# A decoder trunk on one core: sum steps tied to the eighth last low part, attention outputs stored from SyncE's queue, later stick-breaking heads ahead in the order, sums of x two items sooner

## The chip, the cores and the metric

The kernel runs on one core of one Trainium2 chip. The metric is device time in microseconds (us); several executions are timed and the median is taken. One more execution is recorded by the hardware profiler. The core has a matmul engine (PE, its weight loads listed as PEld), a vector engine (DVE), an activation engine (ACT), GpSimd (POOL) and SyncE (SP). SP and POOL issue nearly all DMA transfers, each on a queue of its own (q1 and q0 in the profile), and all transfers run on the same 16 DMA engines.

## The reference, cut to what matters

One layer over 512 tokens of width 1024: three causal attentions side by side, gated, merged and projected, then a squared-ReLU MLP of width 4096 with a gated input embedding; both halves end in a LayerNorm over `alpha * x + ...`. All in 32-bit floats.

```python
def mixer(x, w_in, ...):
    proj = x @ w_in
    (da_q, da_k, da_v, sb_q, sb_k, sb_v, dl_q, dl_k, dl_v, gates) = jnp.split(proj, _split_points(), axis=-1)
    ...
    merged = (g[:, :, 0] * (o_da @ w_branch_da) + g[:, :, 1] * (o_sb @ w_branch_sb)
              + g[:, :, 2] * (o_dl @ w_branch_dil))
    return merged @ w_out

def stick_breaking_attention(q, k, v):
    ...
        z = jnp.einsum('bhqd,bhkd->bhqk', qi, kt).astype(jnp.float32) * scale
        log_keep = jnp.where(before, jax.nn.log_sigmoid(-z), 0.0)
        later = lax.cumsum(log_keep, axis=3, reverse=True) - log_keep
        a = jnp.where(before, jnp.exp(jax.nn.log_sigmoid(z) + later), 0.0)
        return jnp.einsum('bhqk,bhkd->bhqd', a.astype(vt.dtype), vt)

x = LayerNorm(alpha * x + mixer(x))
x = LayerNorm(alpha * x + MLP(x) + sigmoid(x W_g) * (p W_p))
```

## The kernel before

**Products.** Each 32-bit operand is split into a high part, rounded to the matmul's own type, and a low part, the rest. A product is three matmuls: high by high, high by low, low by high (L87 to L89, L562 to L564). Most large products use a seven-product form in the manner of Strassen, for which sums of weight blocks and sums of x are needed.

**Weights.** SP loads raw chunks of 128x1024 (L213, function `fill`) into six `raw` buffers. `split_next` takes each chunk apart: ACT copies the high part (`wh`, L262), DVE subtracts for the low part (`wl`, L264), into rings of five buffers each. `then_add` (L176) lets POOL accumulate a second source onto a raw chunk by DMA.

**Sums of weights.** `sum_steps` forms the sums in DRAM (`vsum`, `qsum`, `msum`, `bsum`, `gsum`, `usum`, `dsum`): 208 steps, each a DMA on POOL, a plain copy (L1241) or an accumulating one (L1239); a step that reads or adds to a sum waits for the step before it on that sum. What spreads them over the run is twofold. In program order, the main loop goes over 321 items (an item is one product with its eviction) and adds to a credit the item's size times its rate; whenever the credit reaches 1, the next step is written down. And each step gets a dependency on `marks[0]`, the oldest of the last low parts noted in `split_next`: with `maxlen=4`, the fourth last.

**Order.** The program order is set by this loop, by generators that are stepped once or twice per item (`pending`, the heads), and by a scheduler that orders each engine's instructions by dependencies and priority. POOL, SP, ACT and DVE each work through their own list in order. `slot` hands out work buffers from a pool; a new tile in a buffer that a DMA store still reads waits for that store.

**The stages around the change.** The three attentions' projections come first; in the third one's value products (about 170 to 230 us) the sums of x (`mixer_forms`: `u7`, `u6`, `u4`, `u5`, casts at L291 and L292) begin at item `forms_at`, and value tiles (`values`) are stored to DRAM by POOL at L519. Eight stick-breaking heads run beside the products (`sb_head`): per key block Abs, Exp and Ln on ACT (L1812 to L1814), a combination on DVE (L1815), its high and low part `sph` (L1818, on ACT for heads 4 to 7) and `spl` (L1819), then on PE the sum over later keys by products with a triangle and with ones (L1844, L1849), and at last Exp (`a`, L1855), `ah` (L1858) and `al` (L1859). `put_away` (L664) stores each of eight attention outputs (`oT4` to `oT11`, 256 KB each) to DRAM from POOL; `bring_back` loads them on SP ahead of the branches. After the branches (about 435 to 620 us) come the output projection (`wout`, L1033 to L1035), whose eviction adds the residual `xn` (loaded by POOL, L1015, used at L1041), the first LayerNorm (its `lr` partly on POOL, L996), and the MLP.

Of the kernel before, what the change touches and what calls it, by code (L numbers as in the profile page):

```python
# [55 lines left out]
def trunk(tc, a, out):  # L56
    nc = tc.nc
    es = ExitStack()
    with es:
# [14 lines left out]
        def slot(name, dt=F32):  # L74
            return big.tile([P, 512], dt, name=nm(name), tag="s", bufs=NSLOT)
# [74 lines left out]
        RING, RAW = 5, 6  # L150
        ORDERED, AHEAD = 17, 4
        loads, chunks, placed = [], [], []
        lows = deque(maxlen=4)
        marks = deque(maxlen=4)
        st = {"dma": 0, "split": 0, "ring": 0}

        def load(src, w, own=False):
# [80 lines left out]
        def split_next():  # L238
            c = chunks[st["split"]]
            w, off = c["w"], c.get("off", 0)  # L240
            if c.get("pre"):
                c["pre"]()
            st["ring"] += not c.get("aside")
            if c.get("apart"):
                hs, ls = [[slot(n, F32R) for _ in range(2)] for n in ("wh", "wl")]
                parts = [(hs[i], ls[i], 512 * i, 512 * i + 512) for i in range(2)]
                c["h"], c["l"] = Halves(hs), Halves(ls)
            elif c.get("beside"):
                h, lo = c["beside"]["tiles"]
                parts = [(h[:, 512:512 + w], lo[:, 512:512 + w], 0, w)]  # L250
                c["h"], c["l"] = parts[0][:2]
            elif c.get("dst") is None:
                h = ring.tile([P, 1024], F32R, name=nm("wh"), tag="wh", bufs=RING)
                lo = ring.tile([P, 1024], F32R, name=nm("wl"), tag="wl", bufs=RING)
                parts = [(h[:, :w], lo[:, :w], 0, w)]
                c["h"], c["l"] = parts[0][:2]
                c["tiles"] = h, lo
            else:
                parts = c["dst"]
            for h, lo, a0, a1 in parts:  # L260
                raw = c["from"]["raw"][:, off + a0:off + a1]
                i = nc.scalar.copy(h, raw)  # L262
                st["cast"] = getattr(i, "ins", i)
                i = nc.vector.tensor_sub(lo, raw, h.bitcast(F32))  # L264
                st["low"] = getattr(i, "ins", i)
                lows.append(st["low"])
                marks.append(st["low"])
            for t in (c["from"], *c.get("also", ())):
                t["uses"] -= 1
            if c.get("then"):  # L270
                c["then"]()
            st["split"] += 1
# [388 lines left out]

        def put_away(k):
            kept_oT[k] = dram.tile([P, 512], F32, name=f"oT{k}")
            nc.gpsimd.dma_start(kept_oT[k], oT.pop(k), max_dma_last_dim=4096)  # L664

        def bring_back(i):
            for k in range(4 * i, 4 * i + 4):
# [60 lines left out]
        def seven(forms, operand, bank_of, done):  # L728

            cs = {}  # L730
            for p in (1, 2, 7, 6, 4, 5, 3):
                for r in range(2):
                    if not r:
                        cs[p] = [operand(cs, p, kp) for kp in range(2)]

                    def mm(ps, p=p, r=r):
                        q = slice(r * P, r * P + P)
                        for k in range(4):
                            c = cs[p][k // 2]
                            n = slice(k % 2 * 512, k % 2 * 512 + 512)  # L740
                            h, lo = forms[p][k]
                            go, end = k == 0 and p in bank_of["first"], k == 3 and p in bank_of["last"]
                            nc.tensor.matmul(ps, h[:, q], c["h"][:, n], start=go, stop=False, skip_group_check=True)  # L743
                            nc.tensor.matmul(ps, h[:, q], c["l"][:, n], start=False, stop=False, skip_group_check=True)  # L744
                            nc.tensor.matmul(ps, lo[:, q], c["h"][:, n], start=False, stop=end, skip_group_check=True)  # L745

                    def bank(p=p, r=r):
                        return bank_of["get"](p, r)

                    def ev(ps, p=p, r=r):  # L750
                        with tc.high_priority():
                            done(ps, p, r)
                    if p == 5:
                        bank_of.get("sums", set()).add(len(items))
                    item(cs[p] if r else [], mm, ev, need=cs[p], bank=bank, size=0.5)
                    items[-1]["rate"] = 1.0

        msum = [[[dram.tile([P, 1024], F32, name=f"msum{n}_{m}_{i}") for i in range(2)] for m in range(2)]
                for n in range(3)]
# [128 lines left out]
        def branch_seven(i, behind):  # L888

            s, b, cs = {}, {}, {}  # L890
            for p in (2, 1, 7, 6, 4, 5, 3):
                for r in range(2):
# [128 lines left out]
        def wout_items():  # L1021
            for half in range(2):
                cs = [chunk(a["wo"][half, c].rearrange("p k n -> p (k n)"), 1024) for c in range(4)]
                for tt in range(4):
# [12 lines left out]
                    def ev(ps, tt=tt, half=half):  # L1037
# [747 lines left out]

        ready = set()

        def sb_head(hd):
            pr, side = hd // 2, hd % 2
            rs = (A, B)[side]  # L1790
# [11 lines left out]
            w = [512, 384, 512]  # L1802
            sph, spl, later = {}, {}, {}
            for bi in (2, 1, 0):
                n = w[bi]
                ps = bank[bi][:, :n]
                e = slot("e")[:, :n]
                with ExitStack() as behind:
                    if hd == 0 and bi == 2:

                        behind.enter_context(tc.issue_after(st["cast"]))
                    nc.scalar.activation(e, ps, AF.Abs)  # L1812
                nc.scalar.activation(e, e, AF.Exp, scale=-1.0)
                ln = nc.scalar.activation(e, e, AF.Ln, bias=1.0)  # L1814
                nc.vector.scalar_tensor_tensor(e, ps, 0.0, e, op0=OP.max, op1=OP.add)  # L1815
                h = slot("sph", F32R)[:, :n]
                lo = slot("spl", F32R)[:, :n]
                (nc.scalar.copy if hd > 3 else nc.vector.tensor_copy)(h, e)  # L1818
                low = nc.vector.tensor_sub(lo, e, h.bitcast(F32))  # L1819
                if hd == 0:  # L1820

                    tie[:] = [getattr(i, "ins", i) for i in (ln, low)]
                sph[bi], spl[bi] = h, lo

                if bi == 2:
                    later[2] = (256, (h[:, HC], lo[:, HC]))
                    sm = slot("sm")[:, HB]
                    nc.vector.tensor_add(sm, e[:, HB], e[:, HC])
                    hl = slot("smp", F32R)
                    nc.vector.tensor_copy(hl[:, HB], sm)  # L1830
                    nc.vector.tensor_sub(hl[:, HC], sm, hl[:, HB].bitcast(F32))
                    later[1] = (256, (hl[:, HB], hl[:, HC]))
                elif bi == 1:
                    nc.vector.tensor_add(e[:, 128:384], e[:, 128:384], sm)
                    h = slot("smh", F32R)[:, :n]
                    lo = slot("sml", F32R)[:, :n]
                    nc.vector.tensor_copy(h, e)
                    nc.vector.tensor_sub(lo, e, h.bitcast(F32))
                    later[0] = (384, (h, lo))
                yield  # L1840
            ah, al = {}, {}
            for kb, bi, c0, n in reversed(blk):
                for hl in (sph, spl) if kb != 2 else ():
                    nc.tensor.matmul(bank[bi][:, :w[bi]], tri_r, hl[bi], start=False, stop=False,  # L1844
                                     skip_group_check=True)
# [12 lines left out]
                (nc.scalar.copy if hd > 3 else nc.vector.tensor_copy)(h, e)  # L1858
                nc.vector.tensor_sub(lo, e, h.bitcast(F32))  # L1859
                ah[bi], al[bi] = h, lo  # L1860
                if kb != 1:
                    yield
# [506 lines left out]
```

## Time and profile before

| | us |
|---|---|
| runs | 1039.46, 1041.79, 1690.32 |
| median | 1041.79 |
| profiled execution | 1041.55 |
| its span, first to last instruction | 1039.8 |
| PE busy | 1019.6 |
| DVE busy | 795.2 |
| ACT busy | 614.1 |
| POOL busy | 213.2 |

The mean granted clock of PE was 0.995. POOL's DMA queue took a share of 51.9% of the 16 DMA engines over the span with 137.18 MB, SP's 35.9% with 136.90 MB. A row of the timeline reads: start, busy time, engine, line, operation, output from input, shape, count, and in brackets the idle time of the engine before it with what ended it. A row of windows reads: window, length, then busy time and count of PE, PEld, DVE, ACT and POOL, the granted clock, the share of the DMA engines and GB/s.

### The profile page before, as it was taken

The numbers are of one execution on the slowest core, as the hardware profiler recorded it, in microseconds if no ns is written. First come the engines' busy times: TensorE is split into PE (matmuls) and PEld (weight loads), VectorE is DVE, ScalarE is ACT, GpSimd is POOL, SyncE is SP. The second block draws the span as 40 slices with busy tenths as digits, with TensorE's granted clock in tenths as the row PEclk, the third lists the DMA queues.
The fourth block names the chain that finished last, engine by engine and source line by source line (L and its number), as shares of the span: only waits on it lengthen the run. The fifth ranks groups of instructions, "written<-read, shape, count | busy, mean of one in ns | idle before, by whom it ended". The sixth has DMA issues, their size and how long they took to land.

```text
span 1039.8 us, 15638 instructions
## 1 busy us (share of the span) xinstructions
PE 1019.6 (98%) x5626; PEld 880.2 (85%) x5626; DVE 795.2 (76%) x1411; ACT 614.1 (59%) x1055; POOL 213.2 (21%) x319
## 2 busy tenths in 40 slices
PE   9999999899999999999999989999999999999997
PEld 7888887688999898888888778788999899899886
DVE  7888679687666876886788795798778777777975
ACT  7565566665444565656654743676666556566651
POOL 1322430112233113111212131221211112111001
PEclk9999999989999999999999999999999999999999
DMA  8999995678899989788999996579999999999722
GB/s 310 297 313 275 260 262 154 199 196 264 278 292 339 255 237 279 202 214 262 334 269 258 301 365 193 122 218 334 343 325 337 323 329 325 343 314 286 248 82 81
DMA packets 79373, 275.99 MB, mean 265 GB/s; under 512 B 9816, under 2 KB 10600, under 8 KB 79296
## 3 DMA queue, kind: packets, MB, share of 16 engines
q0 software_dynamic: 38352, 137.18, 51.9%
q1 hardware_dynamic: 40368, 136.90, 35.9%
q8 instruction: 44, 0.72, 0.3%
q10 hardware_dynamic: 576, 0.92, 0.2%
q14 instruction: 33, 0.27, 0.1%
HBM read 267.59 MB, written 116.42 MB: 369 GB/s over the span
## 4 chain that ended last, share of the span: by engine, by line
PE 77%; DVE 8%; DMA 7%; issue 4%; ACT 3%; POOL 1%; DVEq 0%; SPq 0%; POOLq 0%; ACTq 0%
PE mm L87 9%; PE mm L89 9%; PE mm L88 9%; PE at L1422 4%; PE at L1423 4%; PE at L1424 4%; DVE wl L264 2%; PE at L89 2%; PE at L88 2%; PE at L87 2%; PE mm L743 1%; PE mm L745 1%; PE mm L744 1%; DMA raw<-bsum 1%; DMA raw<-usum 1%
## 5 line engine op out<-in xcount | busy, mean ns | idle before, releaser
L264 DVE TENSOR_TENSOR wl<-raw,wh 128x1024 fp32r<-128x1024 f32 (+1 forms) x274 | 330.3, 1215 | 117.1 <-ACT wh L262 116.1
L262 ACT CAST wh<-raw 128x1024 fp32r<-128x1024 f32 (+1 forms) x274 | 283.6, 1041 | 213.4 <-PE mm L88 99.6
L87 PE MATMUL mm<-xhT,wh 128*128 128x512 f32 (+1 forms) x254 | 95.5, 376 | 0.0
L89 PE MATMUL mm<-xhT,wl 128*128 128x512 f32 (+1 forms) x254 | 94.4, 372 | 0.0
L88 PE MATMUL mm<-xlT,wh 128*128 128x512 f32 (+1 forms) x254 | 94.1, 370 | 0.0
L1422 PE MATMUL at<-wh,hh 128*128 128x512 f32 x188 | 73.7, 392 | 0.0
L1423 PE MATMUL at<-wl,hh 128*128 128x512 f32 x188 | 73.7, 392 | 0.0
L87 PE MATMUL mm<-x1hT,wh 128*128 128x256 f32 x256 | 72.8, 285 | 0.7 <-ACT up L1350 0.7
L1424 PE MATMUL at<-wh,hl 128*128 128x512 f32 x188 | 73.1, 389 | 0.0
L88 PE MATMUL mm<-x1lT,wh 128*128 128x256 f32 x256 | 72.4, 283 | 0.0
L89 PE MATMUL mm<-x1hT,wl 128*128 128x256 f32 x256 | 72.4, 283 | 0.0
L89 PEld LDWEIGHTS mm<-xhT,wl 128*128 128x128 f32 x254 | 47.9, 188 | 8.2
L87 PEld LDWEIGHTS mm<-xhT,wh 128*128 128x128 f32 x254 | 47.9, 189 | 7.8 <-PE mm L596 0.2
L88 PEld LDWEIGHTS mm<-xlT,wh 128*128 128x128 f32 x254 | 47.9, 189 | 7.5
L1239 POOL DMA_DIRECT2D usum<-in_wu_dram x32 | 27.6, 861 | 129.4 <-DVE wl L264 49.0
L87 PEld LDWEIGHTS mm<-x1hT,wh 128*128 128x128 f32 x256 | 48.9, 191 | 2.7 <-ACT up L1350 0.9
L88 PEld LDWEIGHTS mm<-x1lT,wh 128*128 128x128 f32 x256 | 48.9, 191 | 1.5
L89 PEld LDWEIGHTS mm<-x1hT,wl 128*128 128x128 f32 x256 | 48.9, 191 | 0.0
L1239 POOL DMA_DIRECT2D dsum<-in_wd_dram x28 | 23.4, 836 | 118.5 <-DVE wl L264 49.9
L1424 PEld LDWEIGHTS at<-wh,hl 128*128 128x128 f32 x188 | 35.3, 188 | 7.7
L1422 PEld LDWEIGHTS at<-wh,hh 128*128 128x128 f32 x188 | 35.5, 189 | 6.1
L1423 PEld LDWEIGHTS at<-wl,hh 128*128 128x128 f32 x188 | 35.5, 189 | 5.7
(677 smaller groups left out, 2868.8 us busy)
## 6 DMA issues: line engine op xcount, KB each, us to landing
usum<-in_wu_dram POOLq DMA_DIRECT2D x48, 512.0 KB, 9.4
dsum<-in_wd_dram POOLq DMA_DIRECT2D x42, 512.0 KB, 8.8
raw<-usum SPq DMA_DIRECT2D x32, 512.0 KB, 8.6
raw<-dsum SPq DMA_DIRECT2D x28, 512.0 KB, 7.7
raw<-in_wt_dram SPq DMA_DIRECT2D x26, 512.0 KB, 7.3
raw<-in_wd_dram SPq DMA_DIRECT2D x25, 512.0 KB, 6.9
raw<-in_wu_dram SPq DMA_DIRECT2D x24, 512.0 KB, 8.3
qsum<-in_wq_dram POOLq DMA_DIRECT2D x18, 512.0 KB, 9.0
```

The source lines that it names most:

```text
L87: nc.tensor.matmul(ps, wh, xh, start=start, stop=False, skip_group_check=True)
L88: nc.tensor.matmul(ps, wh, xl, start=False, stop=False, skip_group_check=True)
L89: nc.tensor.matmul(ps, wl, xh, start=False, stop=stop, skip_group_check=True)
L262: i = nc.scalar.copy(h, raw)
L264: i = nc.vector.tensor_sub(lo, raw, h.bitcast(F32))
L743: nc.tensor.matmul(ps, h[:, q], c["h"][:, n], start=go, stop=False, skip_group_check=True)
L744: nc.tensor.matmul(ps, h[:, q], c["l"][:, n], start=False, stop=False, skip_group_check=True)
L745: nc.tensor.matmul(ps, lo[:, q], c["h"][:, n], start=False, stop=end, skip_group_check=True)
L1239: i = nc.gpsimd.dma_start(o, i, accum_op=OP.add, max_dma_last_dim=4096)
L1422: nc.tensor.matmul(ps, h[:, q], c["h"][:, s], start=go, stop=False, skip_group_check=True)
L1423: nc.tensor.matmul(ps, h[:, q], c["l"][:, s], start=False, stop=False, skip_group_check=True)
L1424: nc.tensor.matmul(ps, lo[:, q], c["h"][:, s], start=False, stop=end, skip_group_check=True)
```

## The change

Five edits, with no arithmetic added or removed. A sum step depends on the eighth last low part in place of the fourth last. `put_away` no longer issues its store from POOL at once: a generator waits two steps and issues it from SP. The rates change: the items of the seven-product projections from 1.0 to 0.9, those of the branches from 1.0 to 0.7, the output projection's from 1.0 to 2.4. The ACT and DVE work of heads 4 to 7 is written under a raised priority. The sums of x begin at six items ahead of the value stage in place of four.

```diff
-        lows = deque(maxlen=4)
-        marks = deque(maxlen=4)
+        marks = deque(maxlen=8)
...
-                lows.append(st["low"])
                 marks.append(st["low"])
...
         def put_away(k):
             kept_oT[k] = dram.tile([P, 512], F32, name=f"oT{k}")
-            nc.gpsimd.dma_start(kept_oT[k], oT.pop(k), max_dma_last_dim=4096)
+
+            def later():
+                t = oT.pop(k)
+                for _ in range(2):
+                    yield
+                nc.sync.dma_start(kept_oT[k], t)
+            pending.append(later())
...
                     item(cs[p] if r else [], mm, ev, need=cs[p], bank=bank, size=0.5)
-                    items[-1]["rate"] = 1.0
+                    items[-1]["rate"] = 0.9
...
                     item([cs[p]] if r else [], mm, ev, need=[cs[p]], bank=bank, size=0.25)
-                    items[-1]["rate"] = 1.0
+                    items[-1]["rate"] = 0.7
...
                     item(cs if tt == 3 else [], mm, ev, need=cs, bank=at_bank)
+                    items[-1]["rate"] = 2.4
...
+        def ahead(hd):
+            return tc.high_priority() if hd > 3 else ExitStack()
+
         def sb_head(hd):
...
             for bi in (2, 1, 0):
-                n = w[bi]
...
+                with ahead(hd):
+                    n = w[bi]
...
-                nc.scalar.activation(e, bank[bi][:, :n], AF.Exp)
                 h = slot("ah", F32R)[:, :n]
                 lo = slot("al", F32R)[:, :n]
-                (nc.scalar.copy if hd > 3 else nc.vector.tensor_copy)(h, e)
-                nc.vector.tensor_sub(lo, e, h.bitcast(F32))
+                with ahead(hd):
+                    nc.scalar.activation(e, bank[bi][:, :n], AF.Exp)
+                    (nc.scalar.copy if hd > 3 else nc.vector.tensor_copy)(h, e)
+                    nc.vector.tensor_sub(lo, e, h.bitcast(F32))
...
-        forms_at = pair_at[0] - 4
+        forms_at = pair_at[0] - 6
```

In the diff's first loop the whole body of the head's block (Abs, Exp, Ln, the combination, `sph`, `spl` and the sums over keys) moves under `with ahead(hd)`, unchanged.

The lists of the engines show what moves. ACT at the start of the third attention's value products, before: `e_376` and `sph_377` belong to one block of a later head, `wh_394` and `wh_399` are high parts of the weights, `u4h` and `u5h` sums of x.

```order
L291 CAST u4h_365_1837<-xr_359_1808 128x512
L291 CAST u4h_367_1841<-xr_360_1810 128x512
L262 CAST wh_394_1951<-raw_236_1251 128x1024
L1812 ACTIVATE e_376_1880<-at_375_1867 128x512
L262 CAST wh_399_1961<-raw_280_1457 128x1024
L1813 ACTIVATE e_376_1880<-e_376_1880 128x512
L1814 ACTIVATE e_376_1880<-e_376_1880 128x512
L1818 CAST sph_377_1885<-e_376_1880 128x512
L291 CAST u5h_381_1894<-xr_304_1580 128x512
L291 CAST u5h_383_1898<-xr_305_1582 128x512
L569 COPY dl_v_386_1915<-mm_385_1902 128x512
```

The same place on ACT in the changed kernel, where the block's names are `e_380` and `sph_381`:

```order
L1867 ACTIVATE a_370_1847<-at_317_1621 128x512
L1868 CAST ah_371_1848<-a_370_1847 128x512
L1821 ACTIVATE e_380_1888<-at_379_1875 128x512
L1822 ACTIVATE e_380_1888<-e_380_1888 128x512
L1823 ACTIVATE e_380_1888<-e_380_1888 128x512
L1827 CAST sph_381_1893<-e_380_1888 128x512
L261 CAST wh_394_1951<-raw_236_1251 128x1024
L261 CAST wh_399_1961<-raw_280_1457 128x1024
L567 COPY dl_v_386_1915<-mm_385_1902 128x512
```

The block's four instructions stand ahead of both weight casts, and the sums of x have moved to earlier in the list.

POOL at the value stores of the same stage, before (`msum` steps are sums of gate weights, `oT6` is an attention output):

```order
L176 DMA raw_280_1457<-in_wv_dram 128x1024
L176 DMA raw_292_1520<-in_wv_dram 128x1024
L1239 DMA msum0_1_1_98<-in_wgm_dram 128x1024
L519 DMA values0_92<-dl_v_408_1995 128x512
L664 DMA oT6_2011<-oT_342_1741 128x512
L519 DMA values0_92<-dl_v_416_2035 128x512
L1241 DMA msum1_0_0_99<-in_wgm_dram 128x1024
```

And POOL there in the changed kernel:

```order
L1244 DMA msum0_1_1_98<-in_wgm_dram 128x1024
L1246 DMA msum1_0_0_99<-in_wgm_dram 128x1024
L175 DMA raw_280_1457<-in_wv_dram 128x1024
L1246 DMA msum1_1_0_101<-in_wgm_dram 128x1024
L175 DMA raw_296_1527<-in_wv_dram 128x1024
L1246 DMA bsum2_0_111<-in_wbq_dram 128x1024
L517 DMA values0_92<-dl_v_408_1995 128x512
L517 DMA values0_92<-dl_v_416_2034 128x512
```

The accumulating step of `msum0_1_1` now precedes both chunk additions, three plain copies precede the value stores, and the `oT6` store is gone from POOL; on SP it stands between two loads of raw chunks (`raw_445` and `raw_462`).

POOL at the first LayerNorm, before (`lr` is a LayerNorm's factor for one block of tokens, `dsum` sums of the MLP's second weights):

```order
L996 TENSOR_TENSOR lr_1396_6591<-lr_1396_6591,mhalf_272 128x1
L996 TENSOR_TENSOR lr_1401_6631<-lr_1401_6631,mhalf_272 128x1
L176 DMA raw_1353_6371<-in_wg_dram 128x1024
L996 TENSOR_TENSOR lr_1412_6695<-lr_1412_6695,mhalf_272 128x1
L1241 DMA dsum1_3_158<-dsum1_1_156 128x1024
L176 DMA raw_1377_6529<-in_wg_dram 128x1024
L1239 DMA dsum1_3_158<-in_wd_dram 128x1024
L996 TENSOR_TENSOR lr_1420_6741<-lr_1420_6741,mhalf_272 128x1
```

And there in the changed kernel:

```order
L1246 DMA dsum2_0_159<-in_wd_dram 128x1024
L1246 DMA dsum2_2_161<-in_wd_dram 128x1024
L1000 TENSOR_TENSOR lr_1396_6593<-lr_1396_6593,mhalf_272 128x1
L1000 TENSOR_TENSOR lr_1401_6633<-lr_1401_6633,mhalf_272 128x1
L1246 DMA usum4_0_135<-in_wu_dram 128x1024
L175 DMA raw_1353_6367<-in_wg_dram 128x1024
L1000 TENSOR_TENSOR lr_1412_6697<-lr_1412_6697,mhalf_272 128x1
L175 DMA raw_1377_6531<-in_wg_dram 128x1024
L1244 DMA dsum2_0_159<-in_wd_dram 128x1024
L1000 TENSOR_TENSOR lr_1420_6743<-lr_1420_6743,mhalf_272 128x1
```

The copy and the add of `dsum1_3` stand earlier, ahead of the LayerNorm; the add ahead of the last `lr` now belongs to a sum whose copy precedes the first `lr`. Ahead of the eight `xn` loads, earlier in POOL's list, the steps from `dsum1_0`'s add to `usum3_3`'s copy all depend on one low part, where before each had one of its own.

More of the change, by code (lines that the diff above doesn't have):

```diff
@@ L1804, in sb_head @@
             for bi in (2, 1, 0):
-                n = w[bi]
[L1806 to L1837, printed above, removed]
-                    nc.vector.tensor_sub(lo, e, h.bitcast(F32))
-                    later[0] = (384, (h, lo))
+                with ahead(hd):
+                    n = w[bi]
+                    ps = bank[bi][:, :n]
+                    e = slot("e")[:, :n]
+                    with ExitStack() as behind:
+                        if hd == 0 and bi == 2:
+                            behind.enter_context(tc.issue_after(st["cast"]))
+                        nc.scalar.activation(e, ps, AF.Abs)
+                    nc.scalar.activation(e, e, AF.Exp, scale=-1.0)
+                    ln = nc.scalar.activation(e, e, AF.Ln, bias=1.0)
+                    nc.vector.scalar_tensor_tensor(e, ps, 0.0, e, op0=OP.max, op1=OP.add)
+                    h = slot("sph", F32R)[:, :n]
+                    lo = slot("spl", F32R)[:, :n]
+                    (nc.scalar.copy if hd > 3 else nc.vector.tensor_copy)(h, e)
+                    low = nc.vector.tensor_sub(lo, e, h.bitcast(F32))
+                    if hd == 0:
+                        tie[:] = [getattr(i, "ins", i) for i in (ln, low)]
+                    sph[bi], spl[bi] = h, lo
+                    if bi == 2:
+                        later[2] = (256, (h[:, HC], lo[:, HC]))
+                        sm = slot("sm")[:, HB]
+                        nc.vector.tensor_add(sm, e[:, HB], e[:, HC])
+                        hl = slot("smp", F32R)
+                        nc.vector.tensor_copy(hl[:, HB], sm)
+                        nc.vector.tensor_sub(hl[:, HC], sm, hl[:, HB].bitcast(F32))
+                        later[1] = (256, (hl[:, HB], hl[:, HC]))
+                    elif bi == 1:
+                        nc.vector.tensor_add(e[:, 128:384], e[:, 128:384], sm)
+                        h = slot("smh", F32R)[:, :n]
+                        lo = slot("sml", F32R)[:, :n]
+                        nc.vector.tensor_copy(h, e)
+                        nc.vector.tensor_sub(lo, e, h.bitcast(F32))
+                        later[0] = (384, (h, lo))
@@ L1854, in sb_head @@
                 e = slot("a")[:, :n]
-                nc.scalar.activation(e, bank[bi][:, :n], AF.Exp)
                 h = slot("ah", F32R)[:, :n]
                 lo = slot("al", F32R)[:, :n]
-                (nc.scalar.copy if hd > 3 else nc.vector.tensor_copy)(h, e)
-                nc.vector.tensor_sub(lo, e, h.bitcast(F32))
+                with ahead(hd):
+                    nc.scalar.activation(e, bank[bi][:, :n], AF.Exp)
+                    (nc.scalar.copy if hd > 3 else nc.vector.tensor_copy)(h, e)
+                    nc.vector.tensor_sub(lo, e, h.bitcast(F32))
                 ah[bi], al[bi] = h, lo
```

## The prediction

> **What bounds the kernel now.** I read the head of the page and the chain of waits first, then a table of windows over the span, then the timeline of PE wherever a window shows it short of work, and last the timelines of ACT, DVE and POOL just ahead of those places.
>
> ```profile
> span 1039.8 us, 15638 instructions
> PE 1019.6 (98%) x5626; PEld 880.2 (85%) x5626; DVE 795.2 (76%) x1411; ACT 614.1 (59%) x1055; POOL 213.2 (21%) x319
> PE 77%; DVE 8%; DMA 7%; issue 4%; ACT 3%; POOL 1%; DVEq 0%; SPq 0%; POOLq 0%; ACTq 0%
> ...
> 170.00:180.00 10.00, 8.67 (x39) 6.56 (x38) 8.52 (x13) 6.91 (x12) 1.42 (x2) 1.00 0.60 184
> 583.00:606.00 23.00, 19.98 (x88) 15.23 (x87) 16.77 (x21) 16.36 (x25) 3.37 (x5) 1.00 1.04 338
> 1014.00:1039.80 25.80, 18.96 (x96) 16.02 (x95) 15.13 (x35) 4.99 (x12) 4.48 (x6) 0.92 0.22 82
> ```
>
> The matmul engine is busy for 1019.6 of 1039.8 us. The change removes no matmul (the instruction counts of PE are equal in both kernels), so all that it can win is PE's idle time, 20.2 us, and matmuls that ran at a lowered clock. In a windows row the figures are the window, its length, then busy time of PE, PE loads, DVE, ACT and POOL with counts, the granted clock, the DMA share and GB/s. The last row holds 25.80 - 18.96 = 6.8 us of that idle time, in the final LayerNorm, which nothing in the change touches. Some 13 us are left, and they lie in few places: the third attention's value stage around 170 to 209 us, the branches (23.00 - 19.98 = 3.0 us) and one wait behind the first LayerNorm, shown below. The rows of PE in the value stage name the waits:
>
> ```profile
> 177.83 0.50 PE L1844 MATMUL at<-sph,tri_r 128*128 128x512 f32 x1 [1.05 <-ACT sph L1818]
> 178.56 0.50 PE L1844 MATMUL at<-spl,tri_r 128*128 128x512 f32 x1 [0.23 <-DVE spl L1819]
> 194.48 0.50 PE L1844 MATMUL at<-sph,tri_r 128*128 128x512 f32 x1 [0.88 <-ACT sph L1818]
> 203.55 0.50 PE L562 MATMUL mm<-wh,u5h 128*128 128x512 f32 x1 [0.49 <-ACT wh L262]
> 204.81 0.50 PE L563 MATMUL mm<-wl,u5h 128*128 128x512 f32 x1 [0.76 <-DVE wl L264]
> 208.07 0.79 PE L562 MATMUL at<-wh,u4h 128*128 128x512 f32 x1 [2.31 <-DVE dl_v L575]
> ```
>
> The bracket is idle time and what ended it: 5.72 us in all. The lowered clock comes with the last three:
>
> ```profile
> 188.00:192.00 4.00, 4.00 (x20) 3.36 (x20) 3.85 (x7) 3.88 (x6) 2.61 (x5) 1.00 0.84 153
> 204.00:208.00 4.00, 1.01 (x4) 0.48 (x3) 4.00 (x7) 2.98 (x6) 0.52 (x1) 0.79 0.52 171
> 208.00:212.00 4.00, 3.92 (x9) 3.14 (x10) 1.63 (x5) 0.96 (x2) 0.00 (x0) 0.50 0.55 222
> ```
>
> After a window in which PE worked 1.01 us of 4, the granted clock is 0.50 and 9 matmuls fit where 20 did before. Those 9 need 9 x 4.00 / 20 = 1.8 us at the full clock, so the dip costs about 3.92 - 1.8 = 2.1 us beyond the idle time.
>
> **The change part by part.** *Head order and earlier sums of x, first wait.* The head's chain on ACT is Abs, Exp, Ln and the cast to sph, each 0.6 us.
>
> ```profile
> 172.73 1.05 ACT L262 CAST wh<-raw 128x1024 fp32r<-128x1024 f32 x1 [2.27 <-PE at L564]
> 173.68 0.59 ACT L1812 ACTIVATE e<-at 128x512 f32<-128x512 f32 x1
> 174.17 1.04 ACT L262 CAST wh<-raw 128x1024 fp32r<-128x1024 f32 x1
> 177.16 0.62 ACT L1818 CAST sph<-e 128x512 fp32r<-128x512 f32 x1 [0.76 <-DVE e L1815]
> ```
>
> Before, ACT sits 2.27 us behind a weight cast that waits for a ring buffer, and Abs stands behind it. After, the four stand ahead of both casts, and PE's two triangle products stand some 10 us later. Both wh casts now start at most four activations (2.4 us) later; the ring of five covers that if they are ready when the buffer comes free, which the 2.27 us of waiting allows. I take the whole 1.28 us (1.05 + 0.23) as won; bounds 0 and 1.28. At 194.48 three more products, 3 x 0.23 = 0.7 us by the spacing of 20 in 4.00 us, stand ahead of the waiting one: -0.7, bounds 0 and -0.88.
>
> *Stores of attention outputs and value stores.* What makes 203 to 208 late is seen on ACT, DVE and POOL:
>
> ```profile
> 187.76 1.17 POOL L1239 DMA_DIRECT2D msum<-in_wgm_dram  x1
> 189.69 0.58 POOL L519 DMA_DIRECT2D values<-dl_v  x1 [0.77 <-DVE dl_v L572]
> 190.49 0.57 POOL L664 DMA_DIRECT2D oT<-oT  x1 [0.22 <-issue]
> 191.20 0.54 POOL L519 DMA_DIRECT2D values<-dl_v  x1
> ...
> 198.61 0.62 ACT L1858 CAST ah<-a 128x512 fp32r<-128x512 f32 x1 [2.71 <-DMA values<-dl_v]
> 199.93 0.69 DVE L1859 TENSOR_TENSOR al<-a,ah 128x512 fp32r<-128x512 f32 x1 [4.17 <-DMA oT<-oT]
> 201.30 0.60 ACT L1812 ACTIVATE e<-at 128x512 f32<-128x512 f32 x1 [2.06 <-DMA values<-dl_v]
> ```
>
> ACT and DVE want buffers from the slot pool that stores still read: 2.71 + 2.06 us of ACT and 4.17 us of DVE. Everything queued behind them, the casts and low parts of the next chunks among them, comes late, and PE with them. How long transfers took in this stretch (queue, count, size, us to landing):
>
> ```profile
> raw<-in_wv_dram SPq DMA_DIRECT2D x4, 512.0 KB, 6.5
> msum<-in_wgm_dram POOLq DMA_DIRECT2D x4, 512.0 KB, 10.0
> values<-dl_v POOLq DMA_DIRECT2D x2, 256.0 KB, 9.4
> oT<-oT POOLq DMA_DIRECT2D x1, 256.0 KB, 9.3
> ```
>
> Stores of 256 KB on POOL's queue took 9.3 us, loads of twice the size on SP's 6.5. After, the accumulating msum step stands ahead of this place, where the DMA share was 0.60, and only a plain copy and the chunk's own add are still issued just ahead of the value stores; the oT store leaves POOL. I estimate that it lands 9.3 - 6.5 = 2.8 us sooner and the value stores about 2 us sooner (a copy in place of an add ahead of them, taken as a fifth of msum's 10.0 us). That takes 2.0 of the 3.56 us (0.49 + 0.76 + 2.31) from PE: -2.0, bounds 0 and -3.56. For the clock dip I take half, -1.1, bounds 0 and -2.1.
>
> The Trainium skill, "TensorE: Matmul & The Clock Gate", section Part 1 on the HAM clock gate, says that the gate knows half and full alone and falls after a whole window of about 3.4 us without enough work. By that rule the term is all or nothing: the sum would be 1.1 us higher with the dip kept, 1.0 us lower with it gone. The 0.50 above agrees with its half; no row shows the threshold.
>
> *What SP's queue pays.* Eight issues move to SP: it issues the oT store between two weight loads, and is itself in order, so a store that waits for its oT would hold the loads. By the two-step delay the outputs are written before SP comes there; SP's issue takes 0.33 us as its loads' do, and 256 KB at 6.5 / 2 is about 3.3 us of its queue, once per store. Loads run up to six raw buffers ahead, which covers it: 0, bounds 0 and +2 (one of them uncovered by 2 us). POOL's 0.57 us per store goes, off any path.
>
> *Marks and rates.* A sum step waits for the eighth last low part in place of the fourth, so it may start about four chunks earlier; the rates give the branches fewer steps and the output projection more. Where DMA is full and PE busy this moves nothing: 0, bounds -1 and +3 (a chunk's 1.05 us cast late three times). In the branches, loads of summed weights took longest:
>
> ```profile
> raw<-bsum SPq DMA_DIRECT2D x2, 512.0 KB, 14.7
> usum<-in_wu_dram POOLq DMA_DIRECT2D x2, 512.0 KB, 9.6
> ```
>
> By the marks counted in the code, one step fewer runs ahead of the branches' last loads, but four then come together. I take -0.5 of the 3.0 us, bounds +2 and -3.0.
>
> *First LayerNorm.* POOL computes the last lr behind an accumulating step that waits for its copy:
>
> ```profile
> 669.76 0.15 DVE L995 TENSOR_SCALAR lr<-lr 128x1 f32<-128x1 f32 x1
> 670.22 0.85 POOL L1239 DMA_DIRECT2D dsum<-in_wd_dram  x1 [4.42 <-DMA dsum<-dsum]
> 670.80 0.86 POOL L996 TENSOR_TENSOR lr<-lr,mhalf 128x1 f32<-128x1 f32 x1
> 675.58 0.50 PE L1161 MATMUL at<-wh,x1hT 128*128 128x512 f32 x1 [1.09 <-ACT x1r L1083]
> ```
>
> After, the add there belongs to a copy that POOL issues ahead of the first lr, so lr starts at 669.91, 0.9 us sooner: -0.9, bounds 0 and -1.09. Behind it the weight casts are next in line.
>
> Sum: -1.3 - 0.7 - 2.0 - 1.1 + 0 + 0 - 0.5 - 0.9 = -6.5 us. The profiled execution took 1041.55 us (1039.8 span and 1.75 around it), which is 0.24 us under the median of 1041.79; so 1041.55 - 6.5 = 1035.05, said as 1035.
>
> **The rivals.** *The stores land no sooner.* All 16 DMA engines stood at a share of 0.84 at 188 to 192 and more after it; if the share and not the queue sets the landing, 199.93 and 201.30 stay, and with them the terms of 2.0 and 1.1: 1035 + 3.1 = 1038. Against it speaks that 512 KB on SP's queue were faster beside them. The Trainium skill, "DMA: Bandwidth & Descriptors", section "Issuing engines are not separate DMA queues", speaks for it: starting transfers from several engines saves only the time to start them.
>
> *Slower: POOL's burst ahead of the projection's inputs.* POOL works in order, and the steps around the output projection now hang on one low part, the one of 593.57, and come in a row ahead of the xn loads.
>
> ```profile
> 590.17 1.23 DVE L264 TENSOR_TENSOR wl<-raw,wh 128x1024 fp32r<-128x1024 f32 x1 [0.78 <-ACT wh L262]
> 593.57 1.23 DVE L264 TENSOR_TENSOR wl<-raw,wh 128x1024 fp32r<-128x1024 f32 x1 [2.17 <-ACT wh L262]
> 607.22 3.26 POOL L1015 DMA_DIRECT2D xn<-in_xn_dram  x6
> 621.72 0.69 DVE L1041 SCALAR_TENSOR_TENSOR xn<-xn,at 128x512 f32<-128x512 f32 x1
> ```
>
> Two chained waits stand there: an add for its copy, a copy for its add. At 9.6 us each the first xn is issued at 594.8 + 19.2 = 614.0, against 607.22, and with the 9.6 lands at 623.6, 1.9 us after 621.72; one product of the projection (about 6 us, the distance of two such evictions) covers that. At 14.7 us each it is issued at 624.2 and lands at 638.9, 17.2 late, and 17.2 - 6 = 11 us reach PE: 1035 + 11 = 1046. It decides once xn lands after 628. For it: the DMA share of 1.04 there. Against it: loads of 14.7 us were two, and sums in the same stretch took 9.6.
>
> *Nothing moves in sum*: the heads wait for something else by the same amount, each term above at its zero end: 1041.5.
>
> **How the numbers follow.** The forecast has a chance of 0.58, stores no sooner 0.20, the burst 0.15, nothing in sum 0.07. The likeliest gives 1035. Every gain at its end would be 1.28 + 0.88 + 3.56 + 2.1 + 1.0 + 3.0 + 1.09 = 12.9, or 1028.6, which needs all at once, so the range begins at 1030; it ends at 1044, where the zero ends and half of the +2 and +3 lie, and leaves out the burst and some 0.03 below. A change within 2% is about what a measurement of this kernel can't tell from none. A gain of over 2% (21 us) is more than all the idle time that is open: 0.01. Within 2%: 0.96; slower by over 2%: 0.03, a part of the burst.
>
> **What would show it.** Right: no wait for sph or spl near 178; no wait of ACT or DVE for a store of oT near 200; PE's 208 wait under 1.5 us and no 4 us window at clock 0.50; the last lr starting right behind DVE. Wrong: the same buffer waits at the same length; a wait of DVE for xn and PE idle between 610 and 650; ACT waiting for raw where it did not, after a store on SP's queue.

## The result: slower by 1.1%, and the profile after

| | before | changed |
|---|---|---|
| median, us | 1040.55 | 1053.16 |
| lowest, us | 1039.39 | 1047.85 |
| span of the profiled execution, us | 1039.8 | 1052.9 |
| its PE busy time, us | 1019.6 | 1022.7 |

The ratio is 1.0112, with a 95% interval of 1.0075 to 1.0148: slower, by about 12 us. The forecast was 1035 us with a range of 1030 to 1044. Both medians are of five executions, the three listed above among those of the kernel before; the one of 1690.32 us is left out of the ratio, which compares undisturbed executions.

The head of the changed kernel's page:

```profile
span 1052.9 us, 15652 instructions
PE 1022.7 (97%) x5626; PEld 883.4 (84%) x5626; DVE 795.1 (76%) x1411; ACT 615.1 (58%) x1055; POOL 207.7 (20%) x311
PE 75%; DMA 12%; issue 5%; DVE 4%; ACT 2%; POOL 1%; DVEq 0%; POOLq 0%; ACTq 0%
```

The work is the same, but transfers (DMA) have grown from 7% to 12% of the chain that ended last. The span is 13.1 us longer; PE is busy for 3.1 us more with the same number of matmuls, so these ran slower, and idle for 10.0 us more. The main rows of PE's timeline with idle time ahead of them, in the changed kernel:

```profile
133.77 0.80 PE L1878 MATMUL at<-ah,sb_v 128*128 128x512 f32 x1 [5.33 <-DVE ah L1868]
171.92 0.47 PE L87 MATMUL mm<-xhT,wh 128*128 128x512 f32 x1 [2.13 <-DVE dl_k L343]
206.38 0.22 PE L1805 MATMUL at<-mask_b,identb 128*128 128x128 bf16 x1 [0.98 <-ACT dl_v L567]
355.65 0.77 PE L2108 MATMUL at<-pt,dl_vh 128*128 128x256 f32 x1 [7.62 <-DMA dl_vh<-values]
637.49 0.63 PE L947 MATMUL mm<-ident,graw 128*128 128x128 f32 x4 [0.62 <-DVE ml L952]
682.36 0.66 PE L1075 MATMUL at<-ident,xn 128*128 128x128 f32 x4 [1.45 <-ACT ple L1112]
```

The waits for `sph` near 178 and for the weights near 204 are gone, and so are the waits of 3.0 us in the branches (the 0.62 us at 637 is another one, as the experiments show). But two waits stand at places where PE did not wait before: 5.33 us for `ah` and 7.62 us for `dl_vh`, 13 us together. Each is followed by a stretch of lowered clock, as the windows show (the third figure from the end is the granted clock):

```profile
128.00:132.00 4.00, 0.44 (x2) 0.02 (x1) 0.00 (x0) 0.08 (x1) 1.87 (x4) 0.98 0.75 255
132.00:136.00 4.00, 2.23 (x6) 1.61 (x7) 2.68 (x4) 0.00 (x0) 2.62 (x5) 0.50 0.84 186
136.00:140.00 4.00, 4.00 (x15) 3.27 (x14) 3.32 (x8) 0.51 (x1) 2.29 (x3) 0.67 0.92 198
...
352.00:356.00 4.00, 0.34 (x1) 0.38 (x2) 0.00 (x0) 0.00 (x0) 0.85 (x2) 0.50 1.05 314
356.00:360.00 4.00, 4.00 (x14) 3.47 (x14) 0.00 (x0) 0.00 (x0) 0.00 (x0) 0.50 0.90 301
```

**What PE waited for.** Both waits lead to POOL. `rv` is a small bias table that ACT leaves in the work buffer `rvs` and POOL stores to DRAM in five pieces; DVE needs that buffer for `ah` and waits until the stores have read it. In the changed kernel's timeline, DVE first and then POOL:

```profile
133.29 0.43 DVE L1868 CAST ah<-a 128x512 fp32r<-128x512 f32 x1 [8.87 <-DMA rv<-rvs]
...
114.01 0.83 POOL L1244 DMA_DIRECT2D qsum<-in_wq_dram  x1 [11.05 <-DMA qsum<-qsum]
122.37 0.54 POOL L1246 DMA_DIRECT2D qsum<-qsum  x1 [4.28 <-DMA qsum<-in_wq_dram]
125.52 0.52 POOL L1246 DMA_DIRECT2D qsum<-qsum  x1 [2.62 <-DMA qsum<-in_wq_dram]
126.03 2.04 POOL L1673 DMA_DIRECT2D rv<-rvs  x4
```

The brackets of POOL are the point. It waits 11.05 us for a copy of `qsum` to land before it may issue an add to it, then 4.28 and 2.62 us more for such chains, and only then comes to `rv`. Before, the five stores stood ahead of those sums:

```profile
107.11 2.97 POOL L1668 DMA_DIRECT2D rv<-rvs  x5
113.15 0.55 POOL L1241 DMA_DIRECT2D qsum<-qsum  x1 [3.07 <-DVE wl L264]
```

That is 107.11 against 126.03. The loads of `dl_vh`, the values of one head of the third attention, fare alike: before they were issued at 319.96, after at 344.86, behind a row of chained sums (POOL, changed kernel):

```profile
313.64 0.84 POOL L1244 DMA_DIRECT2D msum<-in_wgm_dram  x1 [13.30 <-DMA msum<-msum]
324.19 0.52 POOL L1246 DMA_DIRECT2D bsum<-bsum  x1 [6.38 <-DMA bsum<-in_wbq_dram]
333.00 0.83 POOL L1244 DMA_DIRECT2D bsum<-in_wbq_dram  x1 [4.75 <-DMA bsum<-bsum]
344.34 0.81 POOL L1244 DMA_DIRECT2D msum<-in_wgm_dram  x1 [5.64 <-DMA msum<-msum]
344.86 2.40 POOL L525 DMA_DIRECT2D dl_vh<-values  x3
```

Once issued, they took as long as before. The rows are those of the transfers in a short window around the issue, of the kernel before and of the changed one, the last figure being us to landing:

```profile
dl_vh<-values POOLq DMA_DIRECT2D x3, 256.0 KB, 10.3
```

```profile
dl_vh<-values POOLq DMA_DIRECT2D x3, 256.0 KB, 10.6
```

They are issued 25 us later and need the same time. The five `rv` stores, too, took no longer once issued: 5.0 to 6.4 us, against 9.8 to 10.6 before. So it is the issue that is late, not the transfer. In POOL's list, 41 sum steps now stand ahead of `rv` where 32 stood, and 77 ahead of the third group of `dl_vh` where 67 stood.

### The profile page after: what moved, and what is told of

It reads as the page before. It is cut to its first block, busy times and chain, and to the rows that moved or that the text cites. A ratio compares the mean times of both kernels' runs of the same rounds, so it can differ in the third digit from the quotient of the medians.

```text
span 1052.9 us, 15652 instructions
## 1 busy us (share of the span) xinstructions
PE 1022.7 (97%) x5626; PEld 883.4 (84%) x5626; DVE 795.1 (76%) x1411; ACT 615.1 (58%) x1055; POOL 207.7 (20%) x311
## 4 chain that ended last, share of the span: by engine, by line
PE 75%; DMA 12%; issue 5%; DVE 4%; ACT 2%; POOL 1%; DVEq 0%; POOLq 0%; ACTq 0%
PE mm L87 7%; PE mm L88 7%; PE mm L89 7%; PE at L1427 4%; PE at L1428 4%; PE at L1429 4%; PE at L749 2%; PE at L748 2%; PE at L747 2%; DMA msum<-msum 2%; DMA msum<-in_wgm_dram 2%; PE at L89 2%; PE at L88 2%; PE at L87 2%; PE mm L747 2%
## 5 line engine op out<-in xcount | busy, mean ns | idle before, releaser
L87 PEld LDWEIGHTS mm<-xhT,wh 128*128 128x128 f32 x254 | 48.5, 191 | 10.3 <-issue 2.3
```

What stands on the lines that cost most here:

```text
L87: nc.tensor.matmul(ps, wh, xh, start=start, stop=False, skip_group_check=True)
```

## The experiments

Two theories stood at first. A: the new tie lets sum steps start, and so be ordered, ahead of these small transfers, and POOL, which works through its list in order, holds them while it waits for chained sums. B: the later stores on SP keep work buffers longer, and `dl_vh`, whose buffers now include some that such a store reads, waits for those. All ratios below are to the kernel before, run on the same chip.

**Marks of four in the changed kernel.**

```diff
-        marks = deque(maxlen=8)
+        marks = deque(maxlen=4)
```

> The changed kernel with the sum steps tied to the fourth last low part again, the other four edits kept. Theory A (earlier sum steps stand ahead of the rv stores and of the third group of dl_vh loads in POOL's list, 32 instead of 41 and 67 instead of 77 sum steps ahead of them): PE's waits of 5.33 us at 134 and 7.62 us at 356 go, time 1033 to 1039. Theory B (the attention outputs' later stores on SP keep work buffers longer, and dl_vh waits for those): the wait near 356 stays, time 1046 or more.

Measured: 1038.27 us, ratio 0.9987 (0.9966 to 1.0007). Both waits are gone. The other four edits together give no difference that can be measured.

**Marks of eight in the kernel before**, the same line the other way.

> The kernel before with this one edit: sum steps tied to the eighth last low part. Theory A: both waits are there without any store on SP, time 1048 to 1058. Theory B: no wait of PE over 2 us between 100 and 400, time 1039 to 1043.

Measured: 1059.06 us, ratio 1.0182 (1.0162 to 1.0203). PE's rows of this run:

```profile
110.50 0.79 PE L1871 MATMUL at<-ah,sb_v 128*128 128x512 f32 x1 [6.99 <-DVE ah L1861]
359.44 1.19 PE L2101 MATMUL at<-pt,dl_vh 128*128 128x256 f32 x2 [8.19 <-DMA dl_vh<-values]
531.41 0.76 PE L833 MATMUL mm<-wh,oTh 128*128 128x512 f32 x1 [3.48 <-DVE graw L786]
```

The wait for `dl_vh` is there without any store on SP, so B falls. The first row looks like the other wait and is not: it stands behind these rows of POOL and DVE.

```profile
98.71 0.91 POOL L662 DMA_DIRECT2D oT<-oT  x1
109.55 0.56 DVE L1862 TENSOR_TENSOR al<-a,ah 128x384 fp32r<-128x384 f32 x1 [9.42 <-DMA oT<-oT]
```

`ah` comes right behind this `al`. DVE waits here for the store of an attention output, which POOL issues at 98.71, behind an add that waited 5.73 us for its copy; in the kernel before POOL issued this store at 83.63. `rv` is late too, at 121.74, but nothing waits for it. So theory A holds in kind, with another transfer as the victim. In the changed kernel SP issues this store, at 83.76, and DVE does not wait for it: with marks of eight, the move to SP's queue avoids one loss. The edit loses more alone (1.0182) than in company (1.0113). The third row, a wait in the branches that the changed kernel hasn't, goes with that; the rest of the difference isn't traced.

**The small transfers on SP's queue.** First `rv` alone, then `dl_vh` alone, then both, each in the changed kernel:

```diff
-                nc.gpsimd.dma_start(rv[4 * g:4 * g + 4, d0:d0 + n], sb[r:r + 4, c0:c0 + n])
+                nc.sync.dma_start(rv[4 * g:4 * g + 4, d0:d0 + n], sb[r:r + 4, c0:c0 + n])
...
-                nc.gpsimd.dma_start(t.rearrange("p (c d) -> p c d", c=4), rows)
+                nc.sync.dma_start(t.rearrange("p (c d) -> p c d", c=4), rows)
```

> The changed kernel, only the five small stores of the bias table (rv) issued from SP in place of POOL, so that they pass the sums. Theory A: DVE no longer waits for rv near 133, PE's 5.33 us and the clock dip behind it go, 6 to 8 us in all; the wait near 356 stays; time 1044 to 1049. Theory B (the transfers are late because the DMA engines are full): rv lands as late, time 1050 to 1055.

Measured: 1047.77 us, ratio 1.0080 (1.0049 to 1.0111). The wait of 5.33 us is gone, and the one for `dl_vh` is still 5.79 us.

> The changed kernel, only the twelve loads of dl_vh issued from SP in place of POOL. Theory A: PE's wait of 7.62 us near 356 and the clock dip behind it go, 8 to 10 us in all; the wait near 134 stays; time 1042 to 1047. Theory B (their buffers come free late): SP waits for the buffers in front of weight loads, and PE waits as long or longer, 1052 or more.

Measured: 1049.19 us, ratio 1.0087 (1.0065 to 1.0108), a smaller gain than A gave. The wait for `ah`, which was to stay, fell to 2.32 us, with `rv` issued at 122.38; why isn't shown. SP and PE in this run's timeline:

```profile
322.18 3.45 SPq L525 DMA_DIRECT2D dl_vh<-values  x3
350.72 1.62 PE L2113 MATMUL at<-pt,dl_vh 128*128 128x128 f32 x6 [4.37 <-DMA dl_vh<-values]
```

The transfers around the issue, with us to landing at the end:

```profile
dl_vh<-values SPq DMA_DIRECT2D x3, 256.0 KB, 24.7
```

A window between the two, where the DMA share is the figure before the last:

```profile
326.00:334.00 8.00, 8.00 (x47) 7.01 (x47) 4.95 (x21) 5.31 (x16) 2.37 (x4) 1.00 1.04 320
```

And the window of the kernel before in which POOL issued the same loads:

```profile
318.00:326.00 8.00, 8.00 (x65) 7.84 (x65) 5.61 (x20) 2.80 (x9) 4.24 (x6) 1.00 1.03 264
```

The loads were issued 22.7 us sooner than in the changed kernel and took 24.7 us to land in place of 10.6, so that PE still waited. The full DMA engines alone don't explain that: at a share of 1.03, from POOL's queue, these loads took 10.3 us in the kernel before. The other nine `dl_vh` loads of this run landed from SP's queue in 4.7 to 11.6 us (medians of their groups). What made these three slow isn't shown.

> The changed kernel with both the rv stores and the dl_vh loads issued from SP, so that neither stands behind a sum on POOL; the sums stay tied to the eighth last low part. Theory A1 (only the place in POOL's list costs): both waits end, ratio to the kernel before 0.995 to 1.002. Theory A2 (the sums brought forward also fill the DMA engines, so that the loads land late from any queue; in the run with dl_vh alone on SP they were issued at 322 and PE still waited 4.37 us): the wait for dl_vh stays at 3 to 6 us, ratio 1.003 to 1.008.

Measured: 1044.92 us, ratio 1.0041 (1.0021 to 1.0062). The ratio lies in the range of A2, but by luck: neither form of A described what happened. Both old waits are gone, and a new one stands at an earlier group of `dl_vh`, in rows of SP, ACT and PE:

```profile
279.61 3.27 SPq L525 DMA_DIRECT2D dl_vh<-values  x5
298.24 1.04 ACT L261 CAST wh<-raw 128x1024 fp32r<-128x1024 f32 x1 [9.09 <-DMA raw<-qsum]
299.82 0.47 PE L2098 MATMUL at<-ident,L 128*128 128x128 f32 x1 [5.29 <-ACT pt L96]
```

SP works in order too: five `dl_vh` loads at 279.61 stand ahead of the next raw chunk, ACT waits 9.09 us for that chunk, and PE waits for a copy that stands behind it on ACT.

**Marks of eight from the branches on only.** Steps written before item 108 use the fourth last low part.

```diff
-                tc.add_manual_dep(getattr(i, "ins", i), marks[0].name, mybir.DependencyInfo(
+                tc.add_manual_dep(getattr(i, "ins", i), marks[0 if st["n"] >= gated_at or len(marks) < 4 else -4].name, mybir.DependencyInfo(
```

> The changed kernel, but a sum step written ahead of the branches (items under 108) is tied to the fourth last low part, a later one to the eighth last. Theory A: all of the loss is in the first part, the list of POOL up to the third group of dl_vh is as before, ratio 0.996 to 1.001, no wait over 3 us. Rival (the burst of sums ahead of the output projection costs too): waits of several us between 590 and 690 and ratio above 1.003.

Measured: 1041.25 us, ratio 0.9999 (0.9979 to 1.0019). The loss is in the first part. But one wait of PE misses the "no wait over 3 us", and its rows of POOL, DVE and PE show where it comes from:

```profile
613.02 3.23 POOL L1019 DMA_DIRECT2D xn<-in_xn_dram  x6
620.32 0.69 DVE L1045 SCALAR_TENSOR_TENSOR xn<-xn,at 128x512 f32<-128x512 f32 x1 [6.52 <-DMA xn<-in_xn_dram]
622.37 0.63 PE L947 MATMUL mm<-ident,graw 128*128 128x128 f32 x4 [3.61 <-DVE ml L952]
```

POOL issues the loads of `xn` at 613.02, 12 us later than in the run with marks of four (600.65), after a copy and an add of `dsum` that waited 7.92 and 5.49 us for the step before them; DVE waits 6.52 us for `xn`, and `ml`, which PE needs, stands behind it. This is the prediction's slower rival, at its own place. It is too small to show in the time of this run.

**Four edits less one.** Marks of four, and the sums of x or the rates as before:

```diff
-        forms_at = pair_at[0] - 6
+        forms_at = pair_at[0] - 4
```

> The kernel before with three edits: stores on SP, rates, priority of the later heads; sums of x four items ahead and marks of four as before. If the sums of x two items sooner cause the wait of 2.13 us for dl_k near 164 seen in both kernels that have them, it goes and the wait for sph near 178 returns in part; ratio 0.996 to 0.999. Rival (the priority causes it): it stays.

Measured: 1040.28 us, ratio 0.9987 (0.9969 to 1.0004). The wait for `dl_k` is gone and the value stage is nearly the old one again, so it takes the earlier sums of x to move its waits; without them the raised priority and the store on SP moved hardly any:

```profile
178.01 0.51 PE L1853 MATMUL at<-sph,tri_r 128*128 128x512 f32 x1 [1.05 <-ACT sph L1827]
207.45 0.50 PE L560 MATMUL at<-wh,u4h 128*128 128x512 f32 x1 [2.31 <-DVE dl_v L573]
```

> The kernel before with three edits: stores on SP, priority, sums of x sooner; rates and marks as before. If the rates freed the branches (PE's 3.02 us of idle time between 583 and 606 were gone with marks of four too), these waits return and the 3.3 us at the first LayerNorm fall to about 1; ratio 0.998 to 1.001. Rival (the stores' move freed them): the branches stay free of waits.

Here the three rate edits of the diff are undone. Measured: 1038.96 us, ratio 0.9988 (0.9968 to 1.0008). At the LayerNorm one wait of 1.24 us is left, as expected, but the branches stay without waits, so the rates didn't free them.

**The order alone.** In the changed kernel, marks of eight kept, a sum step written after `rv` or a group of `dl_vh` must also be issued after it.

```diff
-                nc.gpsimd.dma_start(rv[4 * g:4 * g + 4, d0:d0 + n], sb[r:r + 4, c0:c0 + n])
+                i_ = nc.gpsimd.dma_start(rv[4 * g:4 * g + 4, d0:d0 + n], sb[r:r + 4, c0:c0 + n])
+                st["small"] = getattr(i_, "ins", i_)
...
-                nc.gpsimd.dma_start(t.rearrange("p (c d) -> p c d", c=4), rows)
+                i_ = nc.gpsimd.dma_start(t.rearrange("p (c d) -> p c d", c=4), rows)
+                st["small"] = getattr(i_, "ins", i_)
...
-                if plus:
...
+                with tc.issue_after(st["small"]) if "small" in st else ExitStack():
+                    if plus:
...
```

> The changed kernel, sums tied to the eighth last low part as in it, and one addition: a sum step written after the rv stores or a group of dl_vh loads is also issued after them on POOL. No queue, buffer or rate differs; 25 and 64 sum steps stand ahead of rv and of the third dl_vh group in place of 41 and 77. Theory A (the place in POOL's list is the cause): both waits of PE go and no other over 3 us takes their place, ratio to the kernel before 0.995 to 1.002. Rival (sums that run early fill the DMA engines): loads land late all the same, ratio 1.005 or more.

Measured: 1040.82 us, ratio 1.0008 (0.9992 to 1.0025). POOL in this run:

```profile
106.33 2.92 POOL L1675 DMA_DIRECT2D rv<-rvs  x5 [26.55 <-ACT rvs L1671]
313.70 0.75 POOL L525 DMA_DIRECT2D dl_vh<-values  x1 [10.99 <-ACT wh L261]
```

POOL waits here for the small transfers and not they for it, and both waits of PE are gone; a wait of 3.32 us at 624 goes a little over the bound of 3, and it is the one for `xn` again (DVE waits 6.26 us for it), which the addition doesn't touch. With the tie, the queues, buffers and rates of the changed kernel, the place in POOL's list takes back about 11 of the 12 us. The addition also lets the sums it holds back run later, so it changes more than the order of issue; but since the transfers themselves took no longer in the changed kernel, as shown above, the place in the list is what is left as the cause.

**Marks of six in the changed kernel.**

> The changed kernel with the sums tied to the sixth last low part: 36 and 71 sum steps ahead of rv and of the third dl_vh group, about half way between 32 and 41, 67 and 77. Theory A: DVE's wait for rv is between none and 8.9 us and the one of PE for dl_vh between none and 7.6, ratio 1.000 to 1.008. Rival (all or nothing at eight): as with four, 0.997 to 1.000.

Measured: 1036.26 us, ratio 0.9955 (0.9938 to 0.9972), 0.45% faster than the kernel before, and outside what either side expected. Its interval just touches that of marks of four with the same other edits (0.9966 to 1.0007). `dl_vh` is issued at 323.56, 21 us before the changed kernel's, and PE waits for neither it nor `rv`: `rv` is issued at 115.41, 8 us later than in the kernel before, and costs nothing, while 126.03 cost 5.33 us: a later place is free here as long as the consumer has slack, that is, time before it needs the transfer. What the 0.45% comes from isn't shown; its profiled execution was the slowest of its ten (1039.85 us).

**The changed kernel again, and marks of four with the order fixed.**

> The changed kernel itself beside the others on this chip: ratio 1.008 to 1.015, both waits as before. If it were below 1.004, the chip and not the order would have made the first result.

Measured: 1052.21 us, ratio 1.0113 (1.0083 to 1.0143), with waits of 5.13 and 6.26 us.

> The changed kernel with the sums tied to the fourth last low part and the addition of e9_order_only. If the place of these small transfers on POOL limits the kernel before as well, it is faster than with marks of four alone: ratio 0.994 to 0.998. Rival (they were early enough there, as PE waited for neither): 0.997 to 1.001.

Measured: 1039.43 us, ratio 0.9991 (0.9975 to 1.0006), as the rival had it: with marks of four the small transfers were early enough.

## Why the prediction was wrong, by its steps

**Marks and rates.** This is the step that failed. It said that "where DMA is full and PE busy this moves nothing", with bounds of -1 and +3, and priced only a chunk's late cast. It looked at who shares the DMA engines with the sums, not at who stands behind them in POOL's list. The list of the changed kernel had the answer beforehand: `rv` and `dl_vh` are 9 and 10 sum steps further back in it, and a chained step may hold POOL for 3 to 13 us, as the rows above show. Measured, the term is about +13 us: 1.0113 less 0.9987, of 1040 us. PE was busy and the DMA engines full (a share of 1.02 in the window 124 to 128) just where it began, so those two did not keep it at nothing.

**The slower rival** had the right mechanism, chained sums in POOL's list ahead of a load, and it came where it was put, at the `xn` loads, but small. In the changed kernel POOL issues them at 629.24, DVE waits 3.56 us for `xn` at 635.44, and PE 0.62 us at 637.49 for `ml` behind it. That is the sign that the prediction named, a wait of DVE for `xn` and PE idle between 610 and 650; with marks of eight from the branches on it grew to 6.52 and 3.61 us. The runs with marks of four show no wait of DVE there, and neither does the one with marks of eight alone, which has the old rates. The 12 us came from two other places. The same question, asked of every other entry of POOL's list, would have led to them.

**Head order and sums of x.** The waits did go from 177.83 and 178.56, as said; the one of 0.88 fell to 0.45, where -0.7 was forecast. But the sums of x, moved up, now stand on DVE ahead of the eviction `dl_k`, which PE waits for. This is the changed kernel's DVE:

```profile
169.89 1.28 DVE L290 TENSOR_TENSOR u4l<-xr,u4h 128x512 fp32r<-128x512 f32 x2
171.09 0.68 DVE L343 COPY dl_k<-mm 128x512 f32<-128x512 f32 x1
```

And the windows there:

```profile
168.00:172.00 4.00, 1.87 (x15) 1.68 (x15) 3.94 (x7) 3.92 (x8) 0.82 (x1) 1.00 0.35 108
172.00:176.00 4.00, 4.00 (x11) 3.12 (x12) 3.26 (x7) 1.97 (x4) 0.00 (x0) 0.60 0.75 155
```

2.13 us of idle time and a window at clock 0.60 take the place of 1.28 + 0.88 us. By length alone that wait is no heavier, and in some runs no dip follows it (last section). The step named what stands behind the moved casts on ACT, and left out what stands behind the moved sums on DVE.

**Stores on SP.** The oT store was to land 2.8 us sooner and the value stores 2 us. In the changed kernel the transfers of this stretch are these:

```profile
values<-dl_v POOLq DMA_DIRECT2D x2, 256.0 KB, 6.3
oT<-oT SPq DMA_DIRECT2D x1, 256.0 KB, 6.5
```

In the run that has this edit and not marks of eight or the earlier sums of x, these:

```profile
values<-dl_v POOLq DMA_DIRECT2D x2, 256.0 KB, 9.3
oT<-oT SPq DMA_DIRECT2D x1, 256.0 KB, 8.1
```

In the changed kernel the estimate came out: the store gained 2.8 us, the value stores 3.1, and PE's waits there fell from 3.56 to 0.98 us. But the reason given, the queue, is not what the rows show: the value stores, still on POOL, gained as much as the store on SP, and in the other run the two gained 1.2 and 0.1 us and left waits of 0.72 and 2.31 us. So the term was right by luck in part. What shortened the landings isn't shown; in the changed kernel this stage also runs some 8 us later, behind the wait of 5.33 us. The Trainium skill, "DMA: Bandwidth & Descriptors", section "Issuing engines are not separate DMA queues", says that starting DMAs on several engines saves only the time that it takes to start them; 6.5 us on SP beside 6.3 on POOL agrees. What SP's queue pays was put at 0, and no run speaks against it.

**The clock dip** of 208 to 212 did go (in the changed kernel the windows from 196 to 220 are all at 1.00), a gain of about 2.1 us where half was taken. But the waits of 5.33, 7.62 and 2.13 us each brought a dip of their own, and the 3.1 us by which PE's busy time grew are put down to these, by the windows shown.

**The branches** lost the waits that made up their 3.0 us (for `graw` and `b`), against -0.5 predicted; the 0.62 us at 637 is the one for `xn`. They are free of those waits in the run without the rates and in the one without the earlier sums of x as well; what frees them stays open.

**First LayerNorm.** The last `lr` did get its place, and in the changed kernel no `lr` on POOL waits behind a chained add. Yet the waits there rose from 1.09 to 3.17 us (0.62 + 1.45 + 0.59 + 0.51), while the run with marks of eight from the branches on shows none over 0.25. What raised them stays open.

**Range and chances.** The one mechanism that decided was bounded at +3 us, and the range inherited that bound. For a change that reorders a queue holding waits of 3 to 13 us, +3 was no bound. The slower rival's 1046 lay nearest to the 1053 measured, but for a place that cost only 0.62 us.

## What to carry to other kernels

When steps of a background stream are let go earlier, list everything else on the issuing engine's queue that they pass, with the slack of each consumer; a step that waits for the one before it holds all that stands behind it until that one has landed, and what this costs depends on each consumer's slack. An order constraint that keeps a few small, urgent transfers ahead gave back 11 of 12 us here, whereas moving them to another queue put them in front of other urgent loads, or they landed late there. And a setting that steers such a stream is tried in steps: six came out 0.45% below the kernel before, four within the noise of it, eight 1.1% above.

## What the runs showed of the hardware that was not expected

Waits of the same length cost different amounts. The wait of 2.13 us for `dl_k` was followed in the changed kernel by 4 us at a granted clock of 0.60 (11 matmuls where some 20 fit), and so cost nearly twice its length. In the run with marks of eight from the branches on, a wait of 2.14 us at the same instruction was followed by this window, at the full clock and with 19 matmuls:

```profile
164.00:168.00 4.00, 4.00 (x19) 3.27 (x19) 3.26 (x7) 1.86 (x4) 0.00 (x0) 1.00 0.71 145
```

And three 256 KB loads took 24.7 us to land from SP's queue at a DMA share of 1.04, where the same loads took 10.3 us from POOL's in the kernel before at a share of 1.03: neither the size nor the share told the landing time.
